# Loading the sample's memory tiles through GpSimd's queue, with a seventh gate group before the pooling branch

## The chip, the cores and the metric

The kernel runs on one core of a Trainium2 chip. Its engines are TensorE (PE in the profile, with its weight loads as PEld), VectorE (DVE), ScalarE (ACT), GpSimd (POOL) and SyncE (SP, which here only issues transfers). Each engine works through its own list of instructions in order and waits where an instruction needs another engine or a transfer. The metric is the device time of one execution in microseconds (us); the median over runs counts.

## The reference, cut to what matters

One layer of a hybrid decoder, for a prompt of 1024 tokens and for a sample of 8 sequences with 4 new tokens each (32 rows), all with width 1024:

```
h = rmsnorm(x);  pool_in, pool_z, q, k, v, o, z, i/f, gate_a, gate_b = split(h @ w_in)
a  = (multiscale_pool(pool_in) @ pool_w * scale * silu(pool_z)) @ w_pool_down
hc = mlstm(q, k, v, i, f, C0, n0, m0)      # 4 heads of 512, chunks of 128
bm = (head_norm(hc * sigmoid(o)) * silu(z)) @ w_mlstm_down
x  = x + (sigmoid(gate_a) * a + sigmoid(gate_b) * bm) @ w_out
y  = rmsnorm(x + (pe @ w_ple) * sigmoid(rmsnorm(x) @ w_ple_gate))
```

The sample starts from a stored matrix memory: state_mlstm_C holds a 512x512 float32 matrix (1 MB) for each of 8 sequences and 4 heads. Each of these 32 matrices is read, multiplied with the queries, updated with the new keys and values, and written back as new_C_sample.

## The kernel before, in words

Every large product is done in float32 by splitting both operands into a high and a low part and adding three products (mm3, lines 381 to 385). The kernel runs in stages: the input projections for q, k, v, o and z (up to about 890 us), then the gate statistics and the prompt's attention (gates, attn), then the sample's memory (sample, line 1080) beside the pooling branch (pool_branch, line 1199), then the rest of the merge gates, the down projections (downs) and the tail.

The merge gates are sigmoid(h @ w) for 2048 columns, in eight groups of 256 columns (merge_gates, line 1301). One group loads its weights (load_w, line 396), and calls fm (line 437) twice; one fm is three column blocks of 24 matmuls, each block filling one of two PSUM tiles named mm and read out by ACT into a tile sz (line 1311), which is then stored.

Two streams of work are woven together when the program is written. The foreground is merge_gates and pool_branch; the background is a generator (rest, line 1611) that yields after each small piece: 7 pieces of gate statistics, 113 of attention (16 pairs of chunks), 32 steps of the sample, one per 1 MB matrix. After every fm over eight weight tiles, tick (line 456) adds the current rate to a counter and takes as many background pieces as whole numbers it holds. The rate is 1.6 in the statistics, RATE_A = 16 in attention and RATE_S = 1.85 in the sample; a tick adds the rate once, with the value it has when the tick begins. Counted through, the 12 ticks of six gate groups take exactly the 120 pieces of statistics and attention. Then the loop at line 1626 takes one more piece, which closes the attention's SBUF pool and opens the sample's, and pool_branch starts: 16 ticks of 1.85, so that sample steps are spread over all four of its groups (windows of 2, 4, 8 and 16 tokens) and the last ones stand beside gate group 6.

This program order is not yet the order on the engines: the framework sorts each engine's list when the kernel is built, from the program order and its own estimate of when each instruction can run, so later gate blocks can be placed early into an engine's list. On the chip that list is fixed. SBUF is handed out in stacked pools: the pooling branch's pool takes over space of the attention's, so its tiles have to wait until attention has ended.

A sample step (lines 1162 to 1177) makes masked keys km on ACT, loads the matrix into one of three buffers ct, does the matmuls num with it (line 1168), then four times a matmul kv (line 1172) and an update of ct on DVE (line 1173), and stores ct (line 1176). The load into a buffer waits until the store of three steps before has landed. All transfers of the kernel are issued by SP: in sample's stretch these are the loads of ct, the stores of new_C_sample, weights, small outputs of the pooling branch and the pooled result. On POOL lie a few small operations: in attention one per chunk (line 393), in the pooling branch copies and memsets at the edges of the window tiles u (lines 1237 to 1252), on which the window sums on DVE wait.

After the pooling branch, the pool gates3 is opened for gate group 6, the first four tiles of the attention's result (hc_tiles, line 1330; they use the same two buffers sz: load, then a split by ACT and DVE), and gate group 7. Then the down projections begin.

Of the kernel before, what the change touches and what calls it, by code (L numbers as in the profile page):

```python
# [11 lines left out]
F32R = mybir.dt.float32r  # L12
# [6 lines left out]
P = 128  # L19
# [5 lines left out]
H, DH = 4, 512  # L25
# [18 lines left out]
O_GB = O_GA + D  # L44


RATE_A, RATE_S = 16.0, 1.85
HT = T // 2
SH = NS // 2
HH = HT + SH  # L50
# [290 lines left out]
class Trunk:  # L341
# [738 lines left out]
    def sample(self):  # L1080
        nc, I, O = self.nc, self.I, self.O
        a = self.sp
# [59 lines left out]
        for h in range(H):  # L1142

            vf = self.t(a, [P, DH], "voz", bufs=3)[:96]
            for g in range(3):
                nc.sync.dma_start(vf[32 * g:32 * g + 32], self.vSD[h])
            vst = self.t(a, [96, DH], "vst", F32R, bufs=1)
            self.hi(vst, vf)
            self.lo(vst[64:96], vf[64:96], vst[64:96])
            kst = self.t(a, [96, DH], "kst", F32R, bufs=1)  # L1150
            ps = self.miscps()
            for d in range(4):
                nc.tensor.transpose(ps[:NS, d * P:(d + 1) * P], ks[:, h * 4 + d, :], self.ident)
            w = self.wcS[:, h:h + 1]
            self.hi(kst[0:32], ps[:NS, :], w)
            self.lo(kst[32:64], ps[:NS, :], kst[0:32], w)
            nc.scalar.activation(kst[64:96], kst[0:32].bitcast(F32), AF.Copy)

            nc.vector.tensor_copy(qm.rearrange("p (b r) -> p b r", r=132)[:, :, 0:P]
                                  .rearrange("p b (d x) -> p b d x", d=4)[:, :, :, 0:DS],  # L1160
                                  qg[:, h * 4:h * 4 + 4].rearrange("p d (b t) -> p b d t", t=DS))
            for b in range(DB):
                km = self.t(a, [96, DH], "km", F32R, bufs=1)
                nc.scalar.activation(km, kst.bitcast(F32), AF.Identity, scale=self.bcol[:96, b:b + 1])
                ct = self.t(a, [P, 4, DH], "ct", bufs=3)
                nc.sync.dma_start(ct, I["state_mlstm_C"][b, h].rearrange("(d p) e -> p d e", p=P))
                for d in range(4):
                    nc.tensor.matmul(num[32 * d:32 * d + 32, 0, :], lhsT=qm[:, b * P + d * NS:b * P + (d + 1) * NS], rhs=ct[:, d, :],  # L1168
                                     start=b == 0, stop=b == DB - 1)
                for d in range(4):  # L1170
                    kv = self.t(self.ps, [P, 512], "kv", bufs=2)
                    nc.tensor.matmul(kv, lhsT=km[:, d * P:(d + 1) * P], rhs=vst, start=True, stop=True)  # L1172
                    nc.vector.scalar_tensor_tensor(out=ct[:, d, :], in0=ct[:, d, :],  # L1173
                                                   scalar=self.dec[:, h * DB + b, 1:2], in1=kv,
                                                   op0=ALU.mult, op1=ALU.add)
                nc.sync.dma_start(O["new_C_sample"][b, h].rearrange("(d p) e -> p d e", p=P), ct)
                yield True
            nsb = self.t(a, [P, DH], "voz", bufs=3)
            nc.scalar.activation(nsb, num[:, 0, :], AF.Copy)
            nc.tensor.matmul(num[32 * h:32 * h + 32, 1, :], lhsT=self.sel, rhs=nsb, start=True, stop=False)  # L1180
# [367 lines left out]
    def run(self):  # L1548
        ctx, tc = self.ctx, self.tc

        def psum(name, mm, misc):
            st = ExitStack()
            self.nmm, self.nmisc = mm, misc
            self.ps = st.enter_context(tc.tile_pool(name=name, bufs=1, space=PSUM, reuse_waits="tile"))
            return st
        _ps = psum("psA", 0, 2)
        self.dp = ctx.enter_context(tc.tile_pool(name="dram", bufs=1, space=DRAM))
        d = self.dp
        self.qkD = [self.t(d, [P, 8, T], f"qkD{h}") for h in range(H)]
        self.vD = [self.t(d, [T, DH], f"vD{h}") for h in range(H)]  # L1560
        self.oD = [self.t(d, [T, DH], f"oD{h}") for h in range(H)]
        self.zD = [self.t(d, [T, DH], f"zD{h}") for h in range(H)]
        self.hcD = [self.t(d, [P, 4, T], f"hcD{h}") for h in range(H)]
        self.vSD = self.t(d, [H, NS, DH], "vSD")
        self.oSD = self.t(d, [H, NS, DH], "oSD")
        self.zSD = self.t(d, [H, NS, DH], "zSD")
        self.actD = [self.t(d, [P, NT], f"actD{k}") for k in range(KT)]
        self.sgD = [[self.t(d, [P, NT], f"sgD{x}{k}") for k in range(KT)] for x in range(2)]

        self.cp, _c = self.pool("const")  # L1570
        self.qs = self.t(self.cp, [P, 16, NS], "qs")
        self.ks = self.t(self.cp, [P, 16, NS], "ks")
        self.consts()
        self.hp, _h = self.pool("hT", "right")
        self.xp, _x = self.pool("sums", "right")
        self.wp, _w = self.pool("weights1")
        self.gp, _g = self.pool("gemm")
        self.nraw, self.nsb, self.nz = 7, 6, 7
        blocks = []
        for h in range(H):  # L1580
            for kind in "qvkoz":
                if kind in "qk":
                    blocks += [ConvBlock(self, h, kind, g) for g in range(2)]
                else:
                    blocks.append(TokBlock(self, h, kind))
        count = 7 * len(blocks)
        blocks = self.steps(blocks)

        self.norm_in(blocks)
        for n, _ in enumerate(blocks):  # L1590
            if n == count - 10 - 4:
                self.plain_h()
                self.gate_rows()
        _g.close()
        _w.close()
        _x.close()
        _ps.close()
        _ps = psum("ps", 2, 2)
        self.cp2, _c2 = self.pool("const2")
        self.hcS = self.t(self.cp2, [P, H, 4, NS], "hcS")  # L1600
        self.wp, _w = self.pool("weights2")
        self.nraw = 2
        self.mk, _m = self.pool("mask", "right")
        self.masks()
        _m.close()
        self.ap_, _a = self.pool("gates", "right")
        gates = self.gates()
        self.pp, _p = self.pool("gates2")
        _s = []

        def rest():
            self.rate = 1.6
            yield from gates
            _a.close()
            self.atp, _at = self.pool("attn", "right")
            self.attn_setup()
            self.rate = RATE_A
            yield from self.attn()
            _at.close()
            self.sp, st = self.pool("sample", "right")  # L1620
            _s.append(st)
            self.rate = RATE_S
            yield from self.sample()
        self.feed(rest(), 1.6)
        self.merge_gates(range(6))
        while not _s:
            next(self.bg)
        _p.close()
        self.pp, _p = self.pool("poolb")
        self.pool_branch()  # L1630
        _p.close()
        self.mpA, _ma = self.pool("movA")
        self.pp, _p = self.pool("gates3")
        self.merge_gates(range(6, 7))
        first = self.hc_tiles(self.pp, 0, "A", "sz")
        self.merge_gates(range(7, 8))
        self.drain()
        _s[0].close()
        _p.close()
        _h.close()  # L1640
        _ps.close()
        _ps = psum("psD", 6, 2)
        self.mpB, _mb = self.pool("movB", "right")
        self.ep, _e = self.pool("downs")
        self.downs(first)
        _e.close()
        _ma.close()
        self.fp, _f = self.pool("tail")
        self.tail_out()
        _mb.close()  # L1650
        self.lp, _l = self.pool("last", "right")
        self.tail_ple()
        for st in (_l, _f, _w, _c2, _c, _ps):
            st.close()
# [3 lines left out]
           state_mlstm_C=(DB, H, DH, DH), state_mlstm_n=(DB, H, DH), state_mlstm_m=(DB, H), p_prompt=(T, PLE),  # L1658
# [20 lines left out]
```

## Time and profile before

| | us |
|---|---|
| median of 3 runs (2228.46 to 2236.81) | 2232.88 |
| profiled execution | 2232.33 |
| its span | 2230.6 |
| busy: PE / DVE / ACT / POOL | 2159.6 / 1257.2 / 900.8 / 122.7 |

The span is the time from the first to the last instruction of the profiled execution; 1.7 us lie around it. PE is busy for 97% of the span, so that at most about 71 us are idle on it. A busy PE can still run at the lower of its two clocks (1.2 instead of 2.4 GHz), which the column PEclk shows as a mean below 1.00. The DMA queue of the profile carries all 310 MB on one queue.

### The profile page before, as it was taken

The numbers are of one execution on the slowest core, as the hardware profiler recorded it, in microseconds if no ns is written. First come the engines' busy times: TensorE is split into PE (matmuls) and PEld (weight loads), VectorE is DVE, ScalarE is ACT, GpSimd is POOL, SyncE is SP. The second block draws the span as 40 slices with busy tenths as digits, with TensorE's granted clock in tenths as the row PEclk, the third lists the DMA queues.
The fourth block names the chain that finished last, engine by engine and source line by source line (L and its number), as shares of the span: only waits on it lengthen the run. The fifth ranks groups of instructions, "written<-read, shape, count | busy, mean of one in ns | idle before, by whom it ended". The sixth has DMA issues, their size and how long they took to land.

```text
span 2230.6 us, 40176 instructions
## 1 busy us (share of the span) xinstructions
PE 2159.6 (97%) x16407; PEld 2054.8 (92%) x16407; DVE 1257.2 (56%) x2172; ACT 900.8 (40%) x1791; POOL 122.7 (6%) x335
## 2 busy tenths in 40 slices
PE   7999999999999999899999899999988999999998
PEld 6899999999999999899999798787778999999998
DVE  6855576456746565446566675576563243543645
ACT  5645455444635353633333343222223331213443
POOL 1100001000101000000000100000000000000000
PEclk9999999999999999999999999999999999999999
DMA  4233333333233331675655645887774343323112
GB/s 153 85 107 108 102 103 96 108 102 115 93 107 96 112 93 38 195 245 160 196 158 161 204 140 175 294 289 261 252 265 162 97 139 102 108 97 104 53 48 83
DMA packets 238601, 312.72 MB, mean 140 GB/s; under 512 B 13994, under 2 KB 170066, under 8 KB 238416
## 3 DMA queue, kind: packets, MB, share of 16 engines
q1 hardware_dynamic: 238416, 310.15, 42.8%
q8 instruction: 129, 2.11, 0.4%
q14 instruction: 56, 0.46, 0.1%
HBM read 200.01 MB, written 110.45 MB: 139 GB/s over the span
## 4 chain that ended last, share of the span: by engine, by line
PE 87%; DMA 6%; DVE 3%; ACT 2%; SPq 1%; issue 1%; POOL 0%; DVEq 0%; POOLq 0%; ACTq 0%
PE mm L221 21%; PE mm L163 14%; PE mm L383 12%; PE mm L385 12%; PE mm L384 12%; PE num L1168 2%; PE misc L953 2%; PE num L383 1%; PE kv L383 1%; PE num L384 1%; PE num L385 1%; PE kv L384 1%; PE kv L385 1%; PE kv L1172 1%; DMA o<-oD 1%; DMA ct<-state_mlstm_C 1%
## 5 line engine op out<-in xcount | busy, mean ns | idle before, releaser
L376 DVE TENSOR_TENSOR wlo<-wraw,whi 128x1024 fp32r<-128x1024 f32 (+1 forms) x220 | 238.7, 1086 | 228.7 <-ACT whi L370 222.9
L370 ACT ACTIVATE whi<-wraw 128x1024 fp32r<-128x1024 f32 (+1 forms) x220 | 209.2, 951 | 340.8 <-PE mm L221 107.1
L383 PE MATMUL mm<-hh,whi 128*128 128x352 f32 (+1 forms) x832 | 265.7, 319 | 14.5 <-ACT sz L1311 9.0
L385 PE MATMUL mm<-hh,wlo 128*128 128x352 f32 (+1 forms) x832 | 262.6, 316 | 0.0
L384 PE MATMUL mm<-hl,whi 128*128 128x352 f32 (+1 forms) x832 | 261.7, 315 | 0.0
L221 PE MATMUL mm<-wlo,hh 128*128 128x256 f32 x768 | 216.1, 281 | 0.0
L221 PE MATMUL mm<-whi,hl 128*128 128x256 f32 x768 | 215.9, 281 | 0.0
L221 PE MATMUL mm<-whi,hh 128*128 128x256 f32 x768 | 214.6, 279 | 0.0
L383 PEld LDWEIGHTS mm<-hh,whi 128*128 128x128 f32 x832 | 158.8, 191 | 28.5 <-ACT sz L1311 11.3
L384 PEld LDWEIGHTS mm<-hl,whi 128*128 128x128 f32 x832 | 159.2, 191 | 5.7 <-issue 4.4
L385 PEld LDWEIGHTS mm<-hh,wlo 128*128 128x128 f32 x832 | 158.7, 191 | 5.5 <-issue 4.2
L323 DVE SCALAR_TENSOR_TENSOR z<-z,vcols,z 128x556 f32<-128x556 f32 x192 | 146.8, 794 | 8.4 <-ACT z L321 6.6
L163 PE MATMUL mm<-hh,whi 128*128 128x264 f32 x512 | 148.4, 290 | 1.0 <-DVE z L179 0.6
L163 PE MATMUL mm<-hl,whi 128*128 128x264 f32 x512 | 146.2, 286 | 0.4 <-DVE hl L376 0.3
L163 PE MATMUL mm<-hh,wlo 128*128 128x264 f32 x512 | 145.5, 284 | 0.0
L221 PEld LDWEIGHTS mm<-whi,hh 128*128 128x128 f32 x768 | 144.7, 188 | 0.0
L221 PEld LDWEIGHTS mm<-whi,hl 128*128 128x128 f32 x768 | 144.6, 188 | 0.0
L221 PEld LDWEIGHTS mm<-wlo,hh 128*128 128x128 f32 x768 | 144.3, 188 | 0.2
L1173 DVE SCALAR_TENSOR_TENSOR ct<-ct,dec,kv 128x512 f32<-128x512 f32 x128 | 93.4, 744 | 70.9 <-PE kv L1172 61.3
L385 PE MATMUL mm<-mvhB,wlo 128*128 128x352 f32 x384 | 123.2, 322 | 0.0
L384 PE MATMUL mm<-mvlB,whi 128*128 128x352 f32 x384 | 123.0, 322 | 0.0
L383 PE MATMUL mm<-mvhB,whi 128*128 128x352 f32 x384 | 122.1, 324 | 0.0
(462 smaller groups left out, 6071.6 us busy)
## 6 DMA issues: line engine op xcount, KB each, us to landing
wraw<-w_in SPq DMA_DIRECT2D x112, 512.0 KB
ct<-state_mlstm_C SPq DMA_DIRECT2D x32, 1024.0 KB
new_C_sample<-ct SPq DMA_DIRECT2D x32, 1024.0 KB
qkD<-z SPq DMA_DIRECT2D x64, 256.0 KB
qk<-qkD SPq DMA_DIRECT2D x16, 1024.0 KB
sgD<-sz SPq DMA_DIRECT2D x16, 528.0 KB
sg<-sgD SPq DMA_DIRECT2D x16, 528.0 KB
vD<-z SPq DMA_DIRECT2D x32, 256.0 KB
```

The source lines that it names most:

```text
L163: self.tr.nc.tensor.matmul(ps[:, j, :CH], lhsT=st[:, k], rhs=mv[k][:, c], start=start and k == 0 and n == 0, stop=stop and k == 3 and n == ...
L221: self.tr.nc.tensor.matmul(ps[:, t // 2, t % 2 * 256:t % 2 * 256 + 256], lhsT=st[k][:, c], rhs=mv[:, k], start=start and t % 2 == 0 and k ...
L323: nc.vector.scalar_tensor_tensor(out=acc, in0=z[:, o:o + tot], scalar=wc(o), in1=acc, op0=ALU.mult, op1=ALU.add)
L370: self.nc.scalar.activation(out, in_, AF.Copy)
L376: self.nc.vector.tensor_tensor(out=out, in0=in_, in1=hi.bitcast(F32), op=ALU.subtract)
L383: mm(ps, lhsT=sh, rhs=mh, start=start, stop=False)
L384: mm(ps, lhsT=sh, rhs=ml, start=False, stop=False)
L385: mm(ps, lhsT=sl, rhs=mh, start=False, stop=stop)
L953: nc.tensor.matmul(out, lhsT=qk[:, 4 + d, i * L:(i + 1) * L], rhs=qk[:, d, i * L:], start=d == 0, stop=d == 3)
L1168: nc.tensor.matmul(num[32 * d:32 * d + 32, 0, :], lhsT=qm[:, b * P + d * NS:b * P + (d + 1) * NS], rhs=ct[:, d, :], start=b == 0, stop=b = ...
L1172: nc.tensor.matmul(kv, lhsT=km[:, d * P:(d + 1) * P], rhs=vst, start=True, stop=True)
L1173: nc.vector.scalar_tensor_tensor(out=ct[:, d, :], in0=ct[:, d, :], scalar=self.dec[:, h * DB + b, 1:2], in1=kv, op0=ALU.mult, op1=ALU.add)
```

## The change

The loads of ct are issued by GpSimd instead of SP; km gets two buffers instead of one; merge_gates(range(7)) runs before the pooling branch, so that gate group 6 leaves the pool gates3; RATE_S goes from 1.85 to 2.05.

```diff
-RATE_A, RATE_S = 16.0, 1.85
+RATE_A, RATE_S = 16.0, 2.05
...
-                km = self.t(a, [96, DH], "km", F32R, bufs=1)
+                km = self.t(a, [96, DH], "km", F32R, bufs=2)
                 nc.scalar.activation(km, kst.bitcast(F32), AF.Identity, scale=self.bcol[:96, b:b + 1])
                 ct = self.t(a, [P, 4, DH], "ct", bufs=3)
-                nc.sync.dma_start(ct, I["state_mlstm_C"][b, h].rearrange("(d p) e -> p d e", p=P))
+                nc.gpsimd.dma_start(ct, I["state_mlstm_C"][b, h].rearrange("(d p) e -> p d e", p=P))
...
         self.feed(rest(), 1.6)
-        self.merge_gates(range(6))
+        self.merge_gates(range(7))
         while not _s:
             next(self.bg)
...
         self.pp, _p = self.pool("gates3")
-        self.merge_gates(range(6, 7))
         first = self.hc_tiles(self.pp, 0, "A", "sz")
         self.merge_gates(range(7, 8))
```

## Rows read from the trace of the kernel before

**Rows 1.** Part 1 of the page: busy time of PE, share of the span, instructions

```profile
PE 2159.6 (97%) x16407; PEld 2054.8 (92%) x16407; DVE 1257.2 (56%) x2172; ACT 900.8 (40%) x1791; POOL 122.7 (6%) x335
```

**Rows 2.** Stretches: length; PE, PEld, DVE, ACT, POOL busy; PEclk; DMA share, GB/s

```profile
986.00:1176.00 190.00, 190.00 (x1406) 188.03 (x1405) 112.63 (x215) 73.90 (x146) 8.57 (x14) 1.00 0.55 169
1190.00:1240.00 50.00, 44.72 (x319) 41.48 (x319) 32.72 (x65) 20.00 (x41) 2.98 (x4) 0.97 0.59 190
1240.00:1345.00 105.00, 97.72 (x745) 93.44 (x744) 77.03 (x159) 43.26 (x92) 10.03 (x15) 0.97 0.50 156
...
1640.00:1650.00 10.00, 5.46 (x20) 2.67 (x20) 6.54 (x15) 2.05 (x4) 0.00 (x0) 0.66 0.82 270
...
1654.00:1714.00 60.00, 53.16 (x308) 49.90 (x306) 17.82 (x33) 18.57 (x38) 0.55 (x1) 0.94 0.51 176
```

**Rows 3.** The same view in stretches of 10 us: the one that moved most

```profile
1570.00:1580.00 10.00, 10.00 (x53) 7.89 (x52) 1.48 (x2) 1.76 (x4) 0.00 (x0) 1.00 1.04 402
```

**Rows 4.** Timeline of ACT: start, duration; read-outs of gate blocks and the pooling branch's first

```profile
986.02 0.46 ACT L1311 ACTIVATE sz<-mm 128x352 f32<-128x352 f32 x1 [0.88 <-ACT t2k L1054]
...
1175.52 0.45 ACT L1311 ACTIVATE sz<-mm 128x352 f32<-128x352 f32 x1
...
1347.24 0.82 ACT L1219 ACTIVATE sz<-mm 128x352 f32<-128x352 f32 x2
...
1701.06 0.47 ACT L1311 ACTIVATE sz<-mm 128x352 f32<-128x352 f32 x1 [6.34 <-PE mm L385]
1704.87 0.47 ACT L1311 ACTIVATE sz<-mm 128x352 f32<-128x352 f32 x1 [3.35 <-PE mm L385]
```

**Rows 5.** Waits of SP's queue, 1346 to 1672 us: total, times, longest

```profile
SPq L1166 <- DMA new_C_sample<-ct: 101.4, 27, 5.9
```

**Rows 6.** Waits of PE and of its weight loads in the same stretch

```profile
PE num L1168 <- DMA ct<-state_mlstm_C: 6.0, 4, 3.7
...
PE kv L1172 <- ACT km L1164: 1.0, 2, 0.9
...
PEld num L1168 <- DMA ct<-state_mlstm_C: 7.9, 6, 4.0
```

**Rows 7.** Timeline of SP: start, time, issue; small stores ahead of a ct load

```profile
1634.48 4.42 SPq L1299 DMA_DIRECT2D new_pool_sample<-npst  x8
1638.94 0.40 SPq L1166 DMA_DIRECT2D ct<-state_mlstm_C  x1
```

**Rows 8.** DVE's groups, 1347 to 1654 us: busy, mean ns of one | idle before

```profile
L1173 DVE SCALAR_TENSOR_TENSOR ct<-ct,dec,kv 128x512 f32<-128x512 f32 x124 | 90.5, 744 | 61.1 <-PE kv L1172 58.4 <-DMA new_C_sample<-ct 2.3
L1260 DVE TENSOR_TENSOR win<-win 128x276 f32<-128x276 f32 (+5 forms) x48 | 22.5, 470 | 0.5
...
L376 DVE TENSOR_TENSOR pol<-po,poh 128x264 fp32r<-128x264 f32 x32 | 13.7, 427 | 1.2 <-ACT poh L370 1.2
L1264 DVE SCALAR_TENSOR_TENSOR po<-win,u 128x264 f32<-128x264 f32 (+1 forms) x32 | 13.5, 423 | 0.6
```

**Rows 9.** The chain that ended last, in order of time: start, duration

```profile
1474.29 4.34 DMA new_C_sample<-ct
1478.69 5.30 DMA ct<-state_mlstm_C
1484.03 1.06 PE num L1168 x8
...
1670.26 5.57 DMA sz<-hcD
1675.94 1.07 ACT mvhA L370
1677.03 1.24 DVE mvlA L376
```

**Rows 10.** Timeline of PE: start, duration, idle before and its releaser

```profile
1694.41 0.66 PE L383 MATMUL mm<-hh,whi 128*128 128x352 f32 x1 [5.31 <-ACT sz L1311]
```

**Rows 11.** POOL's group with the longest operation: busy, mean ns of one | idle before

```profile
L933 POOL MEMSET C<- 128x2064 f32 x1 | 1.8, 1817 | 0.0
```

## The prediction

> **What bounds the kernel now.** I read the page's busy times first: PE is busy 97% of the span [rows 1], so only its idle time, about 71 us in all, and stretches at the lower clock can be won, and what is moved off or onto the other engines counts only where PE waits for it. Then the stretches [rows 2] show where the change meets such time. While gate blocks lie beside attention (986 to 1176 us) PE is never idle. From 1190 us on they are used up: 5.3 us idle up to 1240, 7.3 us from there to 1345, with a granted clock of 0.97 in both. The timeline of ACT [rows 4] shows why nothing else fills in: the last gate block is read out at 1175.5 us and the first block of the pooling branch only at 1347.2, since its sz needs the attention's SBUF. Later there are two large holes: 4.5 us in the 10 us from 1640, with the clock at 0.66 [rows 2], and 5.3 us before 1694, where gate group 7 waits for a buffer sz [rows 10].
>
> The waits of SP [rows 5] look bad and are not the bound: its ct loads stand at the head of its queue for 101.4 us until a store has landed, but PE waited for ct only 6.0 us [rows 6], 3.7 of them once, where the load was issued behind eight small stores [rows 7].
>
> **What the program order becomes.** I counted ticks in the code. The 13th tick (first half of group 6) adds 16, since its rate is still that of attention when it begins. So it opens the sample and takes 16 of its steps at once; the 14th takes 2. Eighteen of 32 steps then stand ahead of all pooling work instead of one, and the other 14 go two to a tick: the sample ends in the second of four pooling groups instead of beside gate group 6. RATE_S 2.05 alone adds nothing; it sets that pair per tick.
>
> **The sum, part by part**, against the profiled execution (2232.3 us, 0.6 below the median).
>
> *Group 6 beside attention.* It is six blocks of 3.8 us, from one read-out to the next [rows 4], so 22.9 us of PE work; none is added. In the filled stretch 18 blocks went into 190 us [rows 4], 36% of PE. At that share group 6 lasts 63 us, of which 40 us are attention's own: it covers about the stretch 1190 to 1240. That frees 5.3 us idle and 50 x 0.03 = 1.5 us of clock [rows 2]: **-6.8**. Ends: 0, if the holes just reappear later; -17.2 if the blocks spread over the whole tail (12.6 idle, 4.6 clock). I take -6.8, as the filled stretch had no idle time at all. Its weight loads go through SP beside attention as those of groups 0 to 5 do; its sigmoids (0.46 us each) lie on an ACT that is busy less than half the time there.
>
> *The sample gone from pooling group 3.* The hole at 1640 costs 4.5 idle and 10 x 0.34 = 3.4 of clock. PE waits there for a ct load, and the window sums wait on DVE among the sample's updates (0.744 us each [rows 8]). Alone, the group's last chain is four window sums, one difference and one low part: 4 x 0.47 + 0.42 + 0.43 = 2.7 us [rows 8], and two ACT passes of the same width, estimated at 0.42 each: 3.6 us. PE has two blocks of six matmuls under it, 1.9 us at 3.8/24 us per matmul. So 1.7 us stay of 7.9: **-6.2**. Ends: -7.9, and 0 if clock and hole come back at the ends of groups 2 and 3, which then have no sample matmuls in them.
>
> *Gate group 7 without group 6 ahead.* Between the pooling branch and group 7 four tiles pass two buffers sz. Two loads side by side 5.6 us, splits 1.07 + 1.24 + 1.24, two more loads 5.6, two ACT passes [rows 9]: 16.8 us. Group 6 hid all but 5.3 us of this [rows 10]; now PE has only the two blocks that PSUM holds, 7.6 us. Hole 9.2 instead of 5.3: **+3.9**. Ends: -5.3, if the loads can go out before the pooling branch ends; +11.5 if PSUM's two blocks do not go ahead.
>
> *The sample in a burst.* PE needs 1.06 + 4 matmuls kv per step, DVE 4 x 0.744 = 2.98 us, but each step moves 2.1 MB. Before, 124 updates in 307 us [rows 8] are 31 steps, 9.9 us each; at the fastest rate in the trace, 402 GB/s [rows 3], a step needs 5.2 us. A buffer's round is store 4.3, load 5.3, matmul 1.1, updates 3.0 [rows 9, 8]: 13.7 us, or 4.6 per step with three buffers. So a burst is bound by transfers. The waits that come with that are not in the trace at this density. Lower end: 0. Upper end: an order written for DVE's 2.98 us, (5.2 - 2.98) x 18 = 40 us. The nearest row is PE's wait for ct: without the 3.7 us, three of PE's waits make 2.3 us, and six more steps show a wait of the weight load alone [rows 6]: nine tight steps, 0.25 us each. For 32 steps 8.0 less 2.3: **+5.7**.
>
> *POOL's part.* 32 issues leave SP, where they took 0.4 us each [rows 7]. No transfer is issued by POOL before: from 0.4 us up to its longest operation here, 1.8 us [rows 11], which would be 32 x 1.8 = 58 us on an engine that is 6% busy, so nothing on PE, and at most 0.6 us per step within a buffer's round. Behind a waiting load on POOL now stand the edge copies of the pooling branch, and on them the window sums. The wait moves along, 101.4/27 = 3.8 us each, 5.9 at most [rows 5]. Two tiles u and two of PSUM, four blocks of 2.9 us, cover 5.9: zero, inside the upper end above if that cover is gone. SP no longer holds weights and small stores behind ct; PE hardly waited for those.
>
> The Trainium skill ("DMA: Bandwidth & Descriptors", Issuing engines are not separate DMA queues) says that transfers from any engine share the same 16 DMA engines and that a second issuer saves only issue time. By that rule the move of the queue by itself would be worth nothing. SP's row shows that what it lost was waiting, not issuing. The same page (Latency and other measured facts) gives about 1 us to the first byte for GpSimd's path and 0.6 for SyncE's; an estimate from that page is 0.4 us per load, 0.13 us per step, and the sum would be 4 us worse.
>
> *km with two buffers.* PE waited 1.0 us for km [rows 6]; counted as zero, since the updates wait for the same PSUM.
>
> Sum: -6.8 - 6.2 + 3.9 + 5.7 = **-3.4**, so 2228.9 in a profiled run and 2229.5 as median. A measurement of this kernel can tell about 0.5%, 11 us: this is no change.
>
> **The rivals.**
>
> *Everything filled.* The group spreads over the whole tail (-17.2), the pooling branch without the sample loses its hole (-6.2), the tile loads go out early and the burst keeps enough pooling blocks in PE's list (0): -23.4, **2209.5**. For it: 1190 to 1345 has holes in nearly every pair of chunks, and in the later pooling groups DVE is freed. Against it: the blocks are placed as early as possible, as in 986 to 1176.
>
> *PE held by ct loads*, the slower one. Place: the 18 steps ahead of pooling. PE's list is fixed at build; where it sets steps closer than the 5.2 us that transfers need, PE stands in front of each num. It decides from that spacing on. At the buffers' 4.6 us it costs 0.6 x 18 = 11 us, at DVE's 2.98 it is 40; the middle, 26, in place of 5.7 gives 2232.9 - 6.8 - 6.2 + 3.9 + 23.7, **2247**, from 2232 to 2261. For it: the trace has waits on ct at a pace of 9.9 us already. Against it: only three of them without a cause on SP, and all of pooling group 0 is free to stand between.
>
> *Nothing happens*: holes move from 1190 to the next pairs, and the gain at 1640 is lost at the group ends. 2233.
>
> **How the numbers follow.** Forecast 0.46 (its own range 2218 to 2241), everything filled 0.27, held by ct 0.22, nothing 0.05. Faster by over 0.5% (below 2221.7): nearly all of the 0.27 and the lower edge of the forecast, 0.37. Slower (above 2244.0): most of the 0.22 and the forecast's upper edge, 0.20. Within: 0.43. The range 2207 to 2250 leaves out the bottom of the second case and the upper half of the third, under 0.2.
>
> **What would show it.** Right: gate read-outs (L1311) going on to some 1255 us; attention's end later by about 16 us, not 23; steps of the sample 5 to 6.5 us apart; the last new_C_sample store before the third pooling group; under 3 us idle at the end of pooling group 3; a hole of some 9 us before group 7's third block. Wrong: PE's waits on ct above 15 us, or DVE waiting for POOL's copies by more than 6 us at a time (the slower rival); no hole at group 7, or idle time left in attention's tail under 3 us (the faster one).

## The result, and the profile after

The changed kernel takes 2320.4 us (median of four runs, 2317.5 to 2321.4) against 2231.7 us before, measured side by side: a ratio of 1.039 (95% interval 1.037 to 1.041), **89 us slower**. The prediction was 2229.5, its range ended at 2250: wrong, and outside the range.

Parts 1 to 3 of the page of the changed kernel (busy times, granted clock in 40 slices, queues), and the row of the ct loads from its last part, whose end is the median time from issue to landing:

```profile
PE 2200.1 (95%) x16407; PEld 2069.0 (89%) x16407; DVE 1262.6 (54%) x2172; ACT 900.7 (39%) x1791; POOL 144.9 (6%) x367
...
PEclk9999999999999999999999997999598999999999
...
q1 hardware_dynamic: 221520, 276.59, 36.7%
q0 software_dynamic: 8704, 33.56, 4.5%
...
ct<-state_mlstm_C POOLq DMA_DIRECT2D x32, 1024.0 KB, 7.3
```

PE does the same 16407 instructions in a span of 2318.9 us, but is busy 40 us longer [rows 1] and idle 119 us in place of 71. Busy time grows because the clock falls: dents to 7, 5 and 8 tenths, in slices that all stood at 9 before. Stretches of the changed kernel show where they lie (length; PE, PEld, DVE, ACT, POOL busy; granted clock; DMA share, GB/s):

```profile
1190.00:1240.00 50.00, 50.00 (x373) 49.52 (x373) 31.92 (x62) 21.36 (x43) 2.19 (x4) 1.00 0.55 167
...
1398.00:1446.00 48.00, 33.78 (x167) 20.11 (x170) 20.77 (x36) 7.02 (x13) 5.38 (x11) 0.71 0.79 269
1446.00:1612.00 166.00, 158.49 (x965) 124.22 (x957) 91.52 (x172) 44.53 (x88) 18.78 (x43) 0.96 0.76 259
1612.00:1666.00 54.00, 34.19 (x90) 9.94 (x89) 22.04 (x31) 5.57 (x8) 4.50 (x6) 0.53 0.77 272
1666.00:1726.00 60.00, 51.05 (x281) 43.35 (x281) 28.85 (x67) 12.64 (x28) 3.76 (x12) 0.82 0.26 91
1726.00:1765.00 39.00, 36.67 (x252) 34.56 (x252) 29.45 (x74) 12.14 (x31) 4.51 (x13) 0.91 0.25 82
1765.00:1801.00 36.00, 23.42 (x131) 22.84 (x130) 8.31 (x16) 11.74 (x23) 0.00 (x0) 0.81 0.28 96
```

The first row is the part that came as predicted: 1190 to 1240 is full now [rows 2]. Two stretches, 1398 to 1446 and 1612 to 1666, hold 34 us of idle PE, the second at a clock of 0.53. In it PE has 90 matmuls in 54 us, nearly all of them the sample's. DVE is busy 41% there, ACT 10%, the DMA engines 77% at 272 GB/s. Of PE's 20 us of idle time in it 12 are waits on ct, the rest mostly waits on DVE in front of kv. When it is over, the DMA share drops to a quarter and PE does alone the pooling work that had lain beside the sample. The last row is the hole in front of gate group 7.

PE's waits from the first pooling block on (total, times, longest), then POOL's timeline in the second stretch (start, duration, in brackets the idle time before it and its releaser):

```profile
PE num L1168 <- DMA ct<-state_mlstm_C: 30.0, 9, 5.2
PE mm L383 <- ACT sz L1311: 12.6, 2, 11.0
PE kv L1172 <- DVE ct L1173: 8.5, 20, 0.8
PE misc L1102 <- DMA nt<-state_mlstm_n: 3.8, 1, 3.8
```

```profile
1599.99 0.20 POOL L1239 COPY u<-u 128x15 f32<-128x15 f32 x1 [0.78 <-DVE po L1275]
1602.42 0.75 POOL L1166 DMA_DIRECT2D ct<-state_mlstm_C  x1 [2.24 <-DMA new_C_sample<-ct]
...
1656.09 0.76 POOL L1166 DMA_DIRECT2D ct<-state_mlstm_C  x1 [5.26 <-issue]
...
1681.23 0.26 POOL L1239 COPY u<-u 128x15 f32<-128x15 f32 x1 [5.32 <-DVE po L1268]
```

PE waited 6.0 us for ct before [rows 6], now 30.0. Eight loads stand between two edge copies of the pooling branch that are 81 us apart: pooling has stopped. It was not stopped by POOL, though: DVE's wait for those copies is 0.9 us in all.

The reason for the stop stands in PE's list of instructions, which is fixed at build. These are the microseconds of pooling matmuls (0.16 us each for 352 columns, 0.12 for 264) from the first num matmul of one sample step to that of the next; "2 steps a tick" is the run without the burst, below:

```
before            1 8 13 6 5 4 12 4 5 5 9 5 8 2 12 8 7 1 11 3 9 2 8 11 4 6 10 12 1 2 11
after             1 2 19 1 0 0 0 4 5 4 13 3 7 6 7 6 6 3 12 4 6 6 7 5 0 0 0 0 0 0 0
after, on SP      1 1 20 1 0 0 0 4 5 2 10 7 7 2 5 7 5 6 3 10 7 7 2 5 8 1 0 0 0 0 0
2 steps a tick    1 2 20 6 4 5 13 4 4 6 8 6 6 2 9 8 3 6 8 6 6 3 3 9 9 2 6 7 6 6 2
```

Ten gaps are empty in the changed kernel, three in the first stretch and the last seven in the second; DVE's list has no pooling operation in those last seven either. Over the ten empty gaps a step takes 7.8 us from num to num; its 2.1 MB in that time are 269 GB/s, about the rate of the two stretches (269 and 272).

### The profile page after: what moved, and what is told of

The parts are those of the page before. It is cut to its first block, busy times and chain, and to the rows that moved or that the text cites. A ratio compares the mean times of both kernels' runs of the same rounds, so it can differ in the third digit from the quotient of the medians.

```text
span 2318.9 us, 40204 instructions
## 1 busy us (share of the span) xinstructions
PE 2200.1 (95%) x16407; PEld 2069.0 (89%) x16407; DVE 1262.6 (54%) x2172; ACT 900.7 (39%) x1791; POOL 144.9 (6%) x367
## 3 DMA queue, kind: packets, MB, share of 16 engines
q1 hardware_dynamic: 221520, 276.59, 36.7%
q0 software_dynamic: 8704, 33.56, 4.5%
## 4 chain that ended last, share of the span: by engine, by line
PE 84%; DMA 8%; DVE 3%; ACT 2%; issue 1%; SPq 1%; POOL 0%; POOLq 0%; DVEq 0%; ACTq 0%
PE mm L221 20%; PE mm L163 14%; PE mm L383 11%; PE mm L385 11%; PE mm L384 11%; DMA ct<-state_mlstm_C 2%; DMA new_C_sample<-ct 2%; PE misc L953 2%; PE num L1168 2%; PE num L383 1%; PE num L384 1%; PE num L385 1%; PE kv L383 1%; PE kv L384 1%; PE kv L385 1%
```

## The experiments

First come the change's parts in combination. The theories: **order** (the burst leaves PE's list without pooling matmuls, and each bare step lasts as long as its transfers) and **queue** (POOL's queue is the cause). Medians and intervals are each against runs of the kernel before on the same chip.

**The queue alone.**

```
-                nc.sync.dma_start(ct, I["state_mlstm_C"]...
+                nc.gpsimd.dma_start(ct, I["state_mlstm_C"]...
```

> The kernel before with the loads of ct on POOL's queue and nothing else. Order theory (PE's list has stretches of sample steps with no pooling matmuls between them; the queue is secondary): that list is here nearly that of before, with one bare step in 31 instead of ten, so 2232 within 12 us. Queue theory (loads that wait on POOL hold back the copies of the pooling branch, or are slower by themselves): most of the 89 us stays, 2290 to 2325, and PE's waits on ct are above 20 us.

Measured: 2253.2 us, ratio 1.0085 (1.0070 to 1.0100): 19 us slower, between the two. The list is nearly that of before, so the queue costs something by itself, but a fifth of the loss.

**The change with ct on SP.**

```
-                nc.gpsimd.dma_start(ct, I["state_mlstm_C"]...
+                nc.sync.dma_start(ct, I["state_mlstm_C"]...
```

> The changed kernel with the loads of ct back on SP. Order theory: PE's list still has eight bare steps (the changed kernel has ten), so 8/10 of the 89 us stays: 2303, from 2285 to 2325. Queue theory: the loss goes, 2222 to 2242.

Measured: 2294.8 us, 1.0270 (1.0253 to 1.0287). In the order theory's range. Its last five bare steps show the same picture without POOL's queue (stretch and columns as above):

```profile
1589.00:1640.00 51.00, 36.30 (x161) 17.11 (x161) 22.67 (x34) 6.73 (x12) 0.34 (x2) 0.74 0.86 306
```

**The change without the burst**, POOL's queue kept.

```
-            self.rate = RATE_S
+            self.rate, self.acc = RATE_S, 0.0
             yield from self.sample()
```

> The changed kernel, POOL's queue kept, with the sample's credit set to zero where it opens, so that two steps go to a tick and no sixteen at once. PE's list then has pooling matmuls between any two steps. Order theory: the loss goes, 2215 to 2240. Queue theory: it stays above 2285, since the loads still stand ahead of the copies on POOL.

Measured: 2275.2 us, 1.0183 (1.0168 to 1.0198). Between the theories again: no gap of PE's list is empty, and half the loss is gone; PE still waits 28.3 us for ct.

**Neither burst nor POOL's queue** (both edits).

> The changed kernel with both: no sixteen steps at once, loads of ct on SP. What is left of the change is group 6 beside attention, two steps to a tick and two buffers km. Both theories: 2215 to 2240, by the prediction's other terms -6.8 and +3.9 and a sample that is spread. If it is above 2260, something else of the change costs the time (the pair of steps, km, or gate group 7).

Measured: 2247.9 us, 1.0064 (1.0047 to 1.0080): 13 us slower, above the range that both theories gave. The last three runs and the change itself add up. The burst costs 46.9 us with ct on SP (2294.8 less 2247.9) and 45.2 with POOL (2320.4 less 2275.2); the queue costs 25.6 with the burst and 27.4 without; 13 us are something else. (The changed kernel stood beside another set of runs of the kernel before; by the ratios the burst costs 46 and 47 us, the queue 27 and 27.) There are three causes, not one.

What the burst costs on PE can be read from the pages. The lines are those of the change with ct on SP, of the change without the burst, and of the run with neither:

```profile
PE 2184.6 (95%) x16407; PEld 2064.0 (90%) x16407; DVE 1261.9 (55%) x2172; ACT 900.2 (39%) x1791; POOL 120.4 (5%) x335
```

```profile
PE 2169.2 (95%) x16407; PEld 2064.4 (91%) x16407; DVE 1260.5 (55%) x2172; ACT 901.1 (40%) x1791; POOL 146.7 (6%) x367
```

```profile
PE 2161.0 (96%) x16407; PEld 2056.5 (92%) x16407; DVE 1259.5 (56%) x2172; ACT 901.2 (40%) x1791; POOL 121.2 (5%) x335
```

The burst makes PE busy 31 us longer with ct on POOL (2200.1 against 2169.2) and 24 us longer with ct on SP, and idle 15 and 20 us longer. PE's waits on ct grow by only 1.7 us (30.0 against 28.3) and by 9.3 (20.7 against 11.4). So more than half of the burst's cost shows as a slower PE: over the span the granted clock is 0.963 with the burst and 0.977 without, on SP 0.972 and 0.988. In the bare steps themselves the slow clock and the waiting fill the same time, and no run parts them there.

**Is a bare step as long as its transfers?** The change with ct on SP, 31 of the 32 stores left out.

```
-                nc.sync.dma_start(O["new_C_sample"]...
+                if h == 0 and b == 0:
+                    nc.sync.dma_start(O["new_C_sample"]...
```

> The changed kernel with loads of ct on SP (2294.8 us with stores), and of the 32 stores of new_C_sample only the first is left: the other 31 matrices are not written. A step then moves 1.05 MB instead of 2.1, and a buffer is free at once after its last update. PE's list has nine bare steps (eight with stores). Transfer theory (a bare step lasts as long as its transfers): a bare step falls from 7.5 us towards DVE's 2.98, so 2235 to 2262. Order theory (a bare step costs PE its matmuls whatever the transfers do): 2280 to 2300.

Measured: 2261.9 us, 1.0131 (1.0115 to 1.0147), the upper end of the transfer theory. The trace shows eight empty gaps, as many as with the stores; a bare step takes 4.8 us in place of 7.3. The first five of them, and PE's wait on ct from 1405 to 1440 us:

```profile
1408.00:1437.00 29.00, 25.08 (x95) 8.62 (x98) 18.56 (x32) 7.04 (x12) 0.55 (x3) 0.71 0.62 210
```

```profile
PE num L1168 <- DMA ct<-state_mlstm_C: 0.6, 2, 0.4
```

So with the stores the transfers set the length of the bare steps. Without them PE hardly waits for ct there; it is busy 25 of 29 us at a clock of 0.71, so that the step does not fall to DVE's 2.98. The run takes away the bytes of a store and the wait for its landing together and does not part the two. How much is left of the burst can't be read exactly, since the run without burst was not repeated without stores.

**The rest, one: pairs and km**, in the kernel before.

```
-RATE_A, RATE_S = 16.0, 1.85
+RATE_A, RATE_S = 16.0, 2.05
...
-                km = self.t(a, [96, DH], "km", F32R, bufs=1)
+                km = self.t(a, [96, DH], "km", F32R, bufs=2)
```

> The kernel before with RATE_S 2.05 and two buffers km, nothing else. If the 13 us that were left without burst and without POOL's queue come from the pairs of steps: 2240 to 2252. If they come from group 6's move: 2228 to 2238.

Measured: 2233.9 us, 1.0015 (1.0002 to 1.0029): 3 us.

**The rest, two: group 6 alone**, without burst.

```
-            self.rate = RATE_S
+            self.rate, self.acc = RATE_S, 0.0
...
-        self.merge_gates(range(6))
+        self.merge_gates(range(7))
...
-        self.merge_gates(range(6, 7))
```

> The kernel before with group 6 moved beside attention and the credit set to zero where the sample opens; RATE_S 1.85, one buffer km, SP's queue. By the prediction's terms (-6.8 beside attention, +3.9 in front of group 7): 2226 to 2237. If the move itself costs the 13 us (PE's list loses pooling matmuls between the sample's steps): 2241 to 2254.

Measured: 2240.8 us, 1.0035 (1.0022 to 1.0049): 8 us slower, just below the second answer and outside the first. Its stretch 1190 to 1240, and the first waits of PE from 1150 to 1760:

```profile
1190.00:1240.00 50.00, 50.00 (x374) 49.52 (x374) 31.74 (x61) 20.60 (x44) 2.19 (x4) 1.00 0.52 165
```

```profile
PE mm L383 <- ACT sz L1311: 12.8, 2, 11.2
PE num L1168 <- DMA ct<-state_mlstm_C: 12.2, 6, 3.2
```

The 5.3 us in attention are won, and given back twice: 5.9 us more in front of group 7 (11.2 for 5.3), 6.2 us more in front of ct (12.2 for 6.0).

**Was it nt?** In the run with the queue alone PE's waits grew by 11.3 us on ct and by a new one of 7.0 on nt, 18.3 of the 18.6:

```profile
PE num L1168 <- DMA ct<-state_mlstm_C: 17.3, 7, 7.0
PE misc L1102 <- DMA nt<-state_mlstm_n: 7.0, 1, 7.0
```

POOL had issued two loads of 1 MB before SP came to nt's 64 KB, which had been ahead of them. The edit: nt goes to POOL's queue too, in front.

```
-        nc.sync.dma_start(nt, I["state_mlstm_n"]...
+        nc.gpsimd.dma_start(nt, I["state_mlstm_n"]...
```

> The kernel before with the loads of ct on POOL's queue (2253.2 us), and the one load of nt moved to that queue too, ahead of them. PE's wait of 7.0 us on nt should go. If the two waits (7.0 on nt, 11.4 more on ct) make up the 18.6 us: 2243 to 2249. If the wait on nt only hid another one: 2250 to 2256.

Measured: 2250.8 us, 1.0090 (1.0060 to 1.0121). The wait on nt is gone, but the time is in the second answer: it only hid others. PE's waits are now

```profile
PE num L1168 <- DMA ct<-state_mlstm_C: 18.1, 7, 6.8
PE misc L1119 <- DVE qn L1116: 5.5, 1, 5.5
```

**Why are loads from POOL late?** In the run with the queue alone a load lands 5.4 us after its issue at best and 13.8 at most, 7.1 in the middle. For loads that SP issues the page has no such column; the semaphore updates in the trace of the kernel before give 4.9, 10.4 and 5.9. SP's timeline, then POOL's, around a late one: the load of 1424.29 landed only after 10.7 us.

```profile
1418.27 0.38 SPq L1176 DMA_DIRECT2D new_C_sample<-ct  x1
1420.92 0.34 SPq L1289 DMA_DIRECT2D actD<-sz  x1
1422.72 0.38 SPq L1176 DMA_DIRECT2D new_C_sample<-ct  x1
1423.22 0.51 SPq L1289 DMA_DIRECT2D actD<-sz  x1
1424.40 0.37 SPq L404 DMA_DIRECT2D wraw<-pool_w  x1
```

```profile
1424.29 0.75 POOL L1166 DMA_DIRECT2D ct<-state_mlstm_C  x1 [8.12 <-DMA new_C_sample<-ct]
1428.88 0.75 POOL L1166 DMA_DIRECT2D ct<-state_mlstm_C  x1 [3.84 <-DMA new_C_sample<-ct]
```

Here a store, a tile actD, a weight and then the next load are under way with it. The load of this run that had next to nothing beside it (issued at 1441 us) landed in 5.4 us; the four in the kernel before that had nothing beside them landed in 5.3 to 5.6. The same place in the kernel before, SP's timeline:

```profile
1415.02 0.38 SPq L1176 DMA_DIRECT2D new_C_sample<-ct  x1
1416.40 0.37 SPq L1166 DMA_DIRECT2D ct<-state_mlstm_C  x1
1416.87 1.30 SPq L1289 DMA_DIRECT2D actD<-sz  x1
1418.30 0.41 SPq L404 DMA_DIRECT2D wraw<-pool_w  x1
1420.36 0.37 SPq L1166 DMA_DIRECT2D ct<-state_mlstm_C  x1
```

There actD and the weight are issued behind the load that SP had been waiting to issue. That could be the cause, or POOL's path is slow by itself. Two runs were to tell, and did so only half.

```
-                nc.sync.dma_start(O["new_C_sample"]...
+                nc.gpsimd.dma_start(O["new_C_sample"]...
```

> The kernel before with the stores of new_C_sample on POOL's queue, the loads of ct left on SP. Sharing theory (transfers issued by two engines at once share the 16 DMA engines, where those of one engine follow one another, so each load lands later): as with the loads on POOL, PE's waits on ct above 10 us, 2242 to 2258. Path theory (only a load that POOL issues is slow by itself): 2228 to 2238, PE's waits on ct below 6 us.

Measured: 2233.8 us, 1.0009 (0.9997 to 1.0021), no difference, as the path theory said, though PE's wait on ct rose to 9.8 us, which neither theory said. A second queue as such costs nothing that can be measured here.

> The kernel before with loads of ct and stores of new_C_sample both on POOL's queue; weights stay with SP. Sharing theory: a load no longer runs beside a store, only beside weights, so less than the 2253 us of the loads alone: 2236 to 2248, and the loads' median landing time falls from 7.1 us towards 5.4. Path theory: both directions are now slow, 2250 or more.

(The edits of the first run, of the run with nt and of the last one together.) Measured: 2247.1 us, 1.0064 (1.0046 to 1.0081): in the sharing theory's range, but still slow with no store on another queue than the loads; PE waits 14.5 us for ct. The loads' median landing was 6.8 us, hardly less. What is left beside them is weights, voz and actD, and in both slow runs these are on a queue where no load holds them back. So the same question was put without a ct load on POOL, and then with one queue for all. (The order theory in these two is about the order within a queue, no longer about PE's list.)

```
-            nc.sync.dma_start(raw[:, :kk, :n], ap...
+            self.wq.dma_start(raw[:, :kk, :n], ap...
...
-                nc.sync.dma_start(vf[32 * g:32 * g + 32], self.vSD[h])
+                nc.gpsimd.dma_start(vf[32 * g:32 * g + 32], self.vSD[h])
...
-            nc.sync.dma_start(h1, hist...
+            nc.gpsimd.dma_start(h1, hist...
...
-                nc.sync.dma_start(self.actD[ft], sz[f])
+                nc.gpsimd.dma_start(self.actD[ft], sz[f])
...
+        self.wq = self.nc.gpsimd
         self.pool_branch()
+        self.wq = self.nc.sync
```

> The kernel before with the loads of ct and the stores of new_C_sample left on SP, and the other transfers of that stage (weights and history of the pooling branch, voz, actD) on POOL's queue. Order theory (in SP's queue a load of ct that waits holds the other transfers back, and so has the DMA engines to itself when it goes): that protection is gone without any load of ct on POOL, so PE's waits on ct above 10 us and 2240 to 2255. Path theory (only what POOL issues is late): PE's waits on ct stay below 7 us; 2229 to 2237, or more only if PE waits on weights.

Measured: 2248.1 us, 1.0069 (1.0046 to 1.0093), as the order theory said. The second run adds the edits for ct, new_C_sample and nt from above.

> The kernel before with all of these on POOL's queue: loads of ct, stores, nt, weights and history of the pooling branch, voz, actD. Order theory: one queue in order again, so the protection is back: 2230 to 2241, the loads' median landing time below 6.3 us, PE's waits on ct below 9 us. Path theory: everything is late, 2247 or more.

Measured: 2237.8 us, 1.0024 (1.0011 to 1.0036). The time is in the order theory's range, its two other signs were missed by a little: median landing 6.6 us instead of under 6.3, PE's waits on ct 9.8 us instead of under 9. These waits, first with the others on POOL (in the fastest of that run's four executions, 2239.7 us), then with all on POOL (these kernels' lines are one further down):

```profile
PE num L1169 <- DMA ct<-state_mlstm_C: 19.3, 9, 5.6
```

```profile
PE num L1169 <- DMA ct<-state_mlstm_C: 9.8, 4, 3.3
```

With every ct load and store on SP, and only the others moved away, PE waits as long for ct as with the loads on POOL. With all on POOL, in one order again, two thirds of the 16 to 19 us are gone. So it is the **order**: with the loads of ct and the other transfers of this stage in one queue the loss is some 5 us at most, whichever engine issues them; in two queues it is 15 to 19. PE's list is not the reason, since it has nearly the same gaps in the kernel before as with the others on POOL, and with loads and stores on POOL as with all on POOL (as in the table of gaps, whose first row is the kernel before):

```
others on POOL    1 9 13 6 5 3 13 4 5 5 10 6 6 2 11 6 10 1 10 4 7 2 12 7 8 2 11 10 0 2 11
loads and stores  2 6 16 6 3 9 11 4 3 8 8 6 3 13 4 6 6 7 6 6 3 8 11 4 4 10 4 8 1 4 9
all on POOL       1 4 18 6 3 13 4 6 5 8 6 7 2 14 4 6 6 8 6 6 2 10 8 3 5 10 4 8 1 4 9
```

How the one queue does it is argued, not shown: a load that waits at its head would keep what stands behind it off the DMA engines until it has gone. The landing times do not bear this out. In the middle of its 32 loads (for SP's by the semaphore updates) a run has 5.9 us before, 5.7 with the stores on POOL, 6.4 with the others, 6.8 with loads and stores and 7.1 with the loads alone; but with all on POOL it has 6.6, where most of the loss is gone. Nor do the loads go alone in the kernel before: 18 of the last 29 had a transfer that is neither a load of ct nor a store under way beside them, against 17 in the run with the queue alone. The 5 us that stay with all on POOL (2.5 to 8) are the sum of what that move costs and gains; POOL's own part in them is not shown.

**A version that beats both.** A third buffer sz behind the pooling branch, for the hole in front of group 7: in the kernel before, then with the group move.

```
-                z = self.t(self.pp, [P, NT], "sz", bufs=2)
+                z = self.t(self.pp, [P, NT], "sz", bufs=self.gz)
...
-            raw = self.t(pool, [P, NT], tag, bufs=2)
+            raw = self.t(pool, [P, NT], tag, bufs=self.gz)
...
         self.pp, _p = self.pool("gates3")
+        self.gz = 3
...
         self.drain()
+        self.gz = 2
```

> The kernel before with a third buffer sz behind the pooling branch, shared by gate groups 6 and 7 and the four tiles of hc. The hole of 5.3 us in front of group 7 goes: 2225 to 2230. If the fourth tile only moves it to the first blocks behind the gates: 2230 to 2235.

> The group move alone (2240.8 us) with that third buffer sz. Of the hole of 11.2 us three tiles side by side leave some 2: 2229 to 2235, level with the kernel before. If the hole only moves behind the gates: 2237 to 2243. Below 2228 it would beat the kernel before.

Measured: 2225.2 us, 0.9965 (0.9952 to 0.9977), and 2234.7 us, 1.0011 (1.0000 to 1.0023). PE's waits on sz, the one then the other:

```profile
PE mm L384 <- ACT sz L1312: 1.6, 1, 1.6
```

```profile
PE mm L384 <- ACT sz L1312: 7.9, 2, 6.3
```

Both gain 6 us, the second with 6.3 us of its hole left where I expected some 2. The first is the fastest kernel of this study, 6 us below the kernel before by the medians and 8 by the ratio; it takes nothing from the change.

## Why the prediction was wrong

**Group 6 beside attention (-6.8): right.** The stretch 1190 to 1240 is full, and attention ends 17.9 us later (pooling's first read-out at 1365.2, [rows 4] had 1347.2) with 22.9 us of work added: 5.0 won, and 16 us later was forecast. The gate read-outs end at 1240 us, not at 1255.

**The sample gone from pooling group 3 (-6.2): the picture right, the size short.** The last store is issued at 1672.8 us, ahead of that group's first block at 1706.8, and the group's end (1726 to 1765) has no wait on ct; the sample ends in the third group, though (first block at 1566.9), not in the second. But the group's end still loses 2.3 us idle and 9% of the clock over 39 us, 3.5: 5.8 where I had 1.7 left of the hole's 7.9. That the clock comes back at the ends of the groups was my other end, and it was nearer.

**Gate group 7 without group 6 (+3.9): right, a little small.** The hole is 11.0 us, not 9.2. That it was two buffers for four tiles is shown by the third one: it takes 5 us off the hole and 6 off the time. Together with the gates beside attention the sum had -2.9 for the move of group 6; the move alone measured +8. What the sum lacked is a term for the sample: PE's waits on ct grew from 6.0 to 12.2 us. That the gate blocks of group 6 no longer stand beside its last steps is the likely reason, which no run isolates.

**The sample in a burst (+5.7): the step that failed.** It measured 45 to 47. I priced the burst by PE's waits on ct in the kernel before, 0.25 us a step. Those were waits in a list that has pooling matmuls in every gap, so they measured what a late load costs when there is other work, not when there is none. The count of nine tight steps was also misread: four of the six waits of the weight load [rows 6] stand in front of the same steps as PE's four waits. That leaves five steps of 0.45 us, which would have made +12, still far too little. I had the mechanism as a rival, "PE held by ct loads", with 40 us as its end, below what came, and gave it 0.22. Three of its terms were off. A step: 5.2 us at 402 GB/s [rows 3], but that stretch is one of the kernel's fastest; loads and stores side by side moved 259 to 306 GB/s, and a bare step took 7.8. The place: not the 18 steps ahead of the pooling branch, of which only three stand bare, but also the last seven, when the pooling branch had come to a stop. And the clock, which fell to 0.53 where PE had nothing but the sample, and which I had not charged at all: PE's longer busy time is 31 of the 46 us by which the profiled executions differ, on SP 24 of 43. The sample did not get much faster by its burst: 8.9 us from store to store in the mean, 9.4 before. It was PE's other work that was taken out from between its steps and done afterwards alone. Why the build finds no pooling instruction to put there was not tried; that the burst does it is shown by the runs without, whose gaps are all filled.

**POOL's part (0): the second failure.** It measured 19 us alone and 25.6 to 27.4 in this kernel. "SP no longer holds weights and small stores behind ct; PE hardly waited for those" was true, and the wrong question. I asked what had suffered from the wait of 101.4 us [rows 5], not what had profited. What the runs showed in its place is that loads and other transfers in two queues cost 15 to 19 us in the kernel before, and in one queue 5 at most: PE's waits on ct rose from 6.0 to 17.3 us with the loads moved and to 19.3 with the others moved. What the one queue gives the loads stays open, since their landing times alone do not follow the loss. The rule that I weighed in the prediction (the Trainium skill, "DMA: Bandwidth & Descriptors", Issuing engines are not separate DMA queues) says that transfers of all issuers run on the same DMA engines. The trace agrees: a load from POOL landed after 5.4 us with next to nothing beside it, and after up to 13.8 among others. That a second issuer saves only issue time, as the rule goes on, does not say what it can lose, here 19 us. What I feared on POOL, copies held behind waiting loads, did not cost: DVE waited 0.9 us for them.

**Rate and km (0): small.** 3 us, from 0.4 to 6.5; in the changed kernel the pairs without burst and with two km come to 7 (2247.9 less 2240.8).

Of the signs that I had named for being wrong, "PE's waits on ct above 15 us" was the one that came, with 30.0.

## What to carry to other kernels

Before work is moved ahead of other work, ask what will stand in its gaps: a stage that is paced by transfers costs nothing only as long as the busiest engine has something else in its list, and that list can be read before any run. A wait at the head of a DMA queue may look like a loss and be of use: look for what stands behind it, and before transfers that share a queue are parted, part them alone and measure it. And a wait in front of the bound engine is a price only at the density at which it was measured.

## What the hardware showed that was not expected

- The same 1 MB load takes other packets by the issuer: POOL's 32 loads made 8704 packets of the software queue, and the hardware queue has 16896 fewer (238416 less 221520), so 272 to 528 a load. POOL spends 0.75 us on an issue, SP 0.37. With next to nothing beside it, it lands about as soon: 5.4 us from POOL, 5.3 to 5.6 from SP; the best load of the run with the queue alone took 5.4, that of the kernel before 4.9.
- With PE busy 34 of 54 us, its granted clock was 0.53, near the lower of its two levels (1.2 of 2.4 GHz); in the stretch 1446 to 1612, with PE busy 158 of 166, it was 0.96.
- The costs of burst and queue added up within 2 us in the changed kernel. In the kernel before, the queue costs 19 us instead of 26 to 27.
